# Two no-op instructions in GpSimd's program, behind the identity

## The chip, the cores and the metric

One core of one Trainium2 chip. The metric is the device time of one execution in microseconds (us). Beside it, each run lists the span, from the first to the last recorded instruction.

## The reference

A rotary embedding on a tensor of 16 x 512 x 1024, split into 16 heads of 64. The tables cos and sin are 512 x 32.

```python
def reference(x, cos, sin, num_heads):
    batch, seq, dim = x.shape
    x = x.reshape(batch, seq, num_heads, dim // num_heads)
    x1, x2 = x[..., :half], x[..., half:]            # half = 32
    # ... cos and sin get axes for batch and head
    return np.concatenate([x1 * cos - x2 * sin, x1 * sin + x2 * cos], axis=-1)
```

## The kernel before

The batch is cut into 8 tiles of 4 MiB (128 partitions, 8 rows of 1024 each). SyncE issues all transfers. For seven rows of eight, the product with cos is made by VectorE and the one with sin by GpSimd; for the eighth row VectorE makes both. The sum is made by VectorE for three pairs of rows, and by TensorE and ScalarE for the other two rows. The order on each engine is fixed by hand. What the change and the argument touch:

```python
    load(0, 0, FIRST[0])                              # rows 0 to 2 of the first tile
    # ... tabs is a buffer of the pool "b"
    nc.sync.dma_start(out=sin_sb, in_=sin_v)
    nc.sync.dma_start(out=cos_sb, in_=cos_v)
    # ... the rest of tile 0, tiles 1 to 4
    ident = fixed.tile([P, P], FP32)
    make_identity(nc, ident)                          # GpSimd; the change comes behind this
    zero = fixed.tile([P, BANK], BF16)
    # ... spread is made of ident, TensorE spreads the tables over the partitions
    nc.tensor.matmul(out=sin_t, lhsT=spread, rhs=sin_sb, start=True, stop=True)
    nc.tensor.matmul(out=cos_t, lhsT=spread, rhs=cos_sb, start=True, stop=True)
    # ...
    nc.vector.tensor_scalar_mul(out=sns[:, :, 0, :], in0=sin_k, scalar1=-1.0)
    nc.vector.tensor_copy(out=sns[:, :, 1, :], in_=sin_k)
    # ... in sin_product, GpSimd's only work from here on:
        nc.gpsimd.tensor_tensor(out=o, in0=i, in1=sb, op=ALU.mult)
    # ...
    def stores(t):
        if t == 4:
            store_two(3)
        elif t != 3:
            store(t)
        if t == 2:
            load(5)
            load_two(6)                               # tiles 6 and 7
```

## Time and profile before

| | before |
|---|---|
| time, median of 3 runs | 162.64 us (162.54 to 163.0) |
| time and span of the profiled run | 162.73 and 160.5 us |
| transfers | 67.24 MB, 98.0% of 16 engines' span |
| VectorE, GpSimd busy | 85%, 79% |
| GpSimd idle before its first product | 8.40 us |

The first lines to read are shown in the prediction. One more view, two lines of VectorE's part of the list of waits (who waited for whom: us in total, times, longest):

```profile
DVE x L195 <- POOL b L171: 1.5, 1, 1.5
DVE own_ps L147 <- DMA x<-in_x_dram: 0.4, 1, 0.4
```

Once its first products run, VectorE waits twice: once for a product of GpSimd at 21 us, and once, for 0.4 us, for the last load (tiles 6 and 7). The timeline puts that second one at 111 us:

```profile
111.43 1.23 DVE L147 TENSOR_TENSOR own_ps<-x,tab 128x1024 f32<-128x1024 f32 x1 [0.43 <-DMA x<-in_x_dram]
```

From there to its end at 147.87 VectorE has no wait at all.

### The profile page before, as it was taken

The numbers are of one execution on the slowest core, as the hardware profiler recorded it, in microseconds if no ns is written. First come the engines' busy times: TensorE is split into PE (matmuls) and PEld (weight loads), VectorE is DVE, ScalarE is ACT, GpSimd is POOL, SyncE is SP. The second block draws the span as 40 slices with busy tenths as digits, with TensorE's granted clock in tenths as the row PEclk, the third lists the DMA queues.
The fourth block names the chain that finished last, engine by engine and source line by source line (L and its number), as shares of the span: only waits on it lengthen the run. The fifth ranks groups of instructions, "written<-read, shape, count | busy, mean of one in ns | idle before, by whom it ended". The sixth has DMA issues, their size and how long they took to land.

```text
span 160.5 us, 429 instructions
## 1 busy us (share of the span) xinstructions
PE 60.8 (38%) x71; PEld 18.9 (12%) x71; DVE 136.3 (85%) x85; ACT 18.8 (12%) x25; POOL 126.9 (79%) x38
## 2 busy tenths in 40 slices
PE   3043904074505740393109330844057502922000
PEld 0112201030102100120003000300021101210000
DVE  1079879999999999999999999998999999998000
ACT  0003211003100300021101210031003010211000
POOL 1059999999999999988998699982999999960000
PEclk9999995558655675558555955586556755585555
DMA  5999999999999999999999999999999999999993
GB/s 178 410 413 469 392 490 425 392 465 449 392 433 465 408 392 506 408 392 484 425 400 441 465 400 425 474 400 408 490 408 400 474 433 400 465 433 408 433 465 147
DMA packets 2561, 67.25 MB, mean 419 GB/s; under 512 B 256, under 2 KB 384, under 8 KB 384
## 3 DMA queue, kind: packets, MB, share of 16 engines
q1 hardware_dynamic: 2560, 67.24, 98.0%
q14 instruction: 1, 0.01, 0.0%
HBM read 33.69 MB, written 33.55 MB: 419 GB/s over the span
## 4 chain that ended last, share of the span: by engine, by line
DVE 43%; DMA 34%; issue 7%; POOL 7%; PE 1%; SPq 0%; DVEq 0%
DVE x L195 21%; DVE pd L147 18%; DMA x<-in_x_dram 18%; DMA out_dram<-x 12%; POOL b L171 7%; DMA b<-in_sin_dram 4%; DVE pe_ps L147 2%; PE pd L119 1%; DVE sns L122 0%; SPq L77 0%; DVE sns L123 0%; DVE own_ps L147 0%; DVE x L156 0%; DVEq L195 0%; SPq L80 0%
## 5 line engine op out<-in xcount | busy, mean ns | idle before, releaser
L171 POOL TENSOR_TENSOR b<-x,sns 128x2048 f32<-128x2048 f32 (+1 forms) x32 | 126.2, 3980 | 15.5 <-DVE sns L123 8.4
L195 DVE TENSOR_TENSOR x<-pd,b 128x2048 f32<-128x2048 f32 x24 | 54.9, 2286 | 2.3 <-POOL b L171 1.5
L147 DVE TENSOR_TENSOR pd<-x,tab 128x2048 f32<-128x2048 f32 x24 | 55.0, 2291 | 0.2
L182 PE MATMUL own_ps<-x,ident 128*128 128x512 f32 x32 | 30.2, 1099 | 54.9 <-DVE x L156 50.0
L182 PE MATMUL pe_ps<-b,ident 128*128 128x512 f32 x32 | 28.7, 1001 | 23.4 <-DVE pe_ps L147 23.4
L182 PEld LDWEIGHTS own_ps<-x,ident 128*128 128x128 f32 x32 | 9.4, 324 | 74.5 <-DVE x L156 60.6
L215 ACT COPY x<-own_ps 128x1024 f32<-128x1024 f32 x8 | 8.1, 1012 | 75.0 <-PE own_ps L182 75.0
L187 ACT COPY x<-pe_ps 128x512 f32<-128x512 f32 x16 | 9.4, 586 | 37.6 <-PE pe_ps L182 37.6
L182 PEld LDWEIGHTS pe_ps<-b,ident 128*128 128x128 f32 x32 | 8.1, 278 | 42.7 <-DVE pe_ps L147 34.1
L147 DVE TENSOR_TENSOR pe_ps<-x,tab 128x512 f32<-128x512 f32 x16 | 11.0, 686 | 0.0
L147 DVE TENSOR_TENSOR own_ps<-x,tab 128x1024 f32<-128x1024 f32 x8 | 9.8, 1224 | 0.5 <-DMA x<-in_x_dram 0.4
L156 DVE TENSOR_TENSOR x<-x,tab 128x1024 f32<-128x1024 f32 x8 | 9.7, 1213 | 0.0
L122 DVE TENSOR_SCALAR sns<-pd 128x256 f32<-128x256 f32 x1 | 0.4, 425 | 7.3 <-PE pd L119 7.3
L119 PE MATMUL pd<-b,spread 64*128 64x256 f32 x2 | 1.2, 696 | 5.0 <-DMA b<-in_sin_dram 5.0
L215 ACT ACT_TABLE_LOAD x1 | 1.3, 1283 | 14.6 <-DVE x L156 14.6
L107 PE MATMUL own_ps<-zero 128*128 128x512 bf16 x2 | 1.0, 618 | 1.2 <-DVE zero L103 1.2
L119 PEld LDWEIGHTS pd<-b,spread 64*128 64x128 f32 x2 | 0.5, 307 | 5.9 <-issue 5.9
L120 PE MATMUL tab<-b,spread 64*128 64x256 f32 x2 | 1.1, 631 | 0.0
L103 DVE MEMSET zero<- 128x256 uint32 x1 | 0.3, 272 | 0.9 <-PEq L246 0.9
L120 PEld LDWEIGHTS tab<-b,spread 64*128 64x128 f32 x2 | 0.7, 333 | 0.2
L107 PE MATMUL pe_ps<-zero 128*128 128x512 bf16 x1 | 0.6, 631 | 0.0
L107 PEld LDWEIGHTS <-zero 128*128 128x128 bf16 x3 | 0.3, 123 | 1.5 <-DVE zero L103 1.2
(9 smaller groups left out, 1.8 us busy)
## 6 DMA issues: line engine op xcount, KB each, us to landing
out_dram<-x SPq DMA_DIRECT2D x6, 4096.0 KB, 22.1
x<-in_x_dram SPq DMA_DIRECT2D x2, 8192.0 KB, 38.8
x<-in_x_dram SPq DMA_DIRECT2D x3, 4096.0 KB, 27.9
out_dram<-x SPq DMA_DIRECT2D x1, 8192.0 KB, 33.2
x<-in_x_dram SPq DMA_DIRECT2D x1, 2560.0 KB, 11.4
x<-in_x_dram SPq DMA_DIRECT2D x1, 1536.0 KB, 6.4
b<-in_sin_dram SPq DMA_DIRECT2D x1, 64.0 KB, 6.3
b<-in_cos_dram SPq DMA_DIRECT2D x1, 64.0 KB, 6.1
```

Source lines behind the costliest of these rows:

```text
L103: nc.vector.memset(zero, 0.0)
L107: nc.tensor.matmul(out=ps, lhsT=zero[:, :P], rhs=zero, start=True, stop=True)
L119: nc.tensor.matmul(out=sin_t, lhsT=spread, rhs=sin_sb, start=True, stop=True)
L120: nc.tensor.matmul(out=cos_t, lhsT=spread, rhs=cos_sb, start=True, stop=True)
L122: nc.vector.tensor_scalar_mul(out=sns[:, :, 0, :], in0=sin_k, scalar1=-1.0)
L147: nc.vector.tensor_tensor(out=o, in0=i, in1=cb, op=ALU.mult)
L156: nc.vector.tensor_tensor(out=heads(r), in0=heads(r), in1=s, op=ALU.mult)
L171: nc.gpsimd.tensor_tensor(out=o, in0=i, in1=sb, op=ALU.mult)
L182: nc.tensor.matmul(out=ps, lhsT=ident, rhs=other, start=False, stop=True, skip_group_check=True)
L187: nc.scalar.copy(out=r, in_=pe_ps)
L195: nc.vector.tensor_tensor(out=r, in0=ps, in1=b, op=ALU.add)
L215: nc.scalar.copy(out=r0, in_=own_ps)
```

## The change

It adds two instructions that compute nothing. As its intent one can read: a small pause of GpSimd, to see whether its place in time matters.

```diff
     ident = fixed.tile([P, P], FP32)
     make_identity(nc, ident)
+    for _ in range(2):
+        nc.gpsimd.nop(hint="pause")
     zero = fixed.tile([P, BANK], BF16)
```

## The prediction

> **What bounds the kernel now.** I read the summary first, then the slices of the transfer engines, then the waits of the engine that gets the new instructions, then the chain to the end. The summary and the slices:
>
> ```profile
> span 160.5 us, 429 instructions
> PE 60.8 (38%) x71; PEld 18.9 (12%) x71; DVE 136.3 (85%) x85; ACT 18.8 (12%) x25; POOL 126.9 (79%) x38
> ...
> DMA  5999999999999999999999999999999999999993
> ...
> q1 hardware_dynamic: 2560, 67.24, 98.0%
> ```
>
> What to see: the row "DMA" is in its top tenth in 38 of 40 slices, and the one data queue fills 98.0% of the span of all 16 transfer engines. The kernel reads 32 MiB and writes 32 MiB, plus small tables: 67.24 MB. I cut the span into stretches to get a rate without head and tail: 433 GB/s from 10 to 148 us. 67.24 MB at 433 GB/s is 155.3 us, and the span is 160.5. So about 5 us of the span is head (transfers begin between 1 and 2 us and run at a reduced rate until 3) and tail (nothing moves after 159). The time is the data volume at a flat rate, with one important companion: VectorE, which is busy for 136.3 us and nearly without a gap from 10 us to 147.9. It finishes the last tile at 147.9, the last store of 4 MiB is issued then, and 4.19 MB at 433 GB/s are 9.7 us of the 12.6 that remain. The transfer share in 148 to 157 us is still 0.97. So the two arrive at the end together: the queue has hardly any backlog when VectorE is done, and a real delay of VectorE late in the program would be seen in the time.
>
> Now GpSimd, whose program is the only one changed. Its timeline around the place of the change (start, length, line, operation, and in brackets how long it was idle and for what):
>
> ```profile
> 0.73 0.20 POOL masks.py:197 MEMSET ident<- 128x128 f32 x1 [0.29 <-POOLq L246]
> 1.01 0.29 POOL masks.py:199 TENSOR_SCALAR_AFFINE_SELECT ident<-ident 128x128 f32<-128x128 f32 x1
> 9.71 47.26 POOL L171 TENSOR_TENSOR b<-x,sns 128x2048 f32<-128x2048 f32 x12 [8.40 <-DVE sns L123]
> ```
>
> The identity is done at 1.30 us. The next GpSimd instruction starts at 9.71, and all 8.40 us between are a wait for VectorE's copy of the sine table. Why that comes so late is in the chain:
>
> ```profile
> 1.17 6.34 DMA b<-in_sin_dram
> 7.51 0.14 issue
> 7.64 1.20 PE pd L119 x2
> 8.85 0.02 issue
> 8.87 0.42 DVE sns L122
> 9.30 0.34 DVE sns L123
> 9.64 0.07 issue
> 9.71 4.14 POOL b L171
> ```
>
> The sine table lands 6.34 us after its issue, TensorE spreads it over the partitions, VectorE makes the negated and the plain half, and 0.07 us later GpSimd starts. GpSimd has no part in this chain between 1.30 and 9.64 us. The identity itself is an early input of it (VectorE copies it into the spreading matrix at 1.34 us, for 0.22 us), but that copy is ready at 1.56 and TensorE needs it only at 7.6.
>
> [...] The trace of the kernel before has no such instruction[...]. [...] The nearest thing in the trace is SyncE's semaphore instructions that did not have to wait: 17 to 28 ns. [...]
>
> **The change part by part.** It removes nothing and moves nothing. I compared the two programs as built, on every engine: TensorE, VectorE, ScalarE and SyncE have the same instructions in the same order with the same waits, but for the line numbers, which rise by two. GpSimd's listing gains one row, two no-ops between the identity's select and the first sine product. The waits of every later product are those of before; the no-ops wait for nothing and nothing waits for them.
> - Cost on GpSimd's sequencer: 2 times 17 to 28 ns from the row above, so 34 to 56 ns. If a no-op cost ten times that[...] it would be 0.6 us.
> - What lies in the way: they run after 1.30 us, or even earlier, as the sequencer may be ahead of the engine, and are over by 1.4 us (1.9 in the tenfold case). GpSimd has nothing to do before 9.64 us. Spare time: 8.40 us against 0.06. It would take about 8.40 / 0.028 = 300 such no-ops to fill the gap.
> - What comes out on the path: 0.00 us. The sum is the time of before, 162.64 us.
>
> **The rivals.**
> First: the no-ops delay the first sine product, because they hold the sequencer until the engine is empty or the sequencer reaches the wait late. For it: VectorE does depend on these products (it waited 1.5 us for one at 21 us). Against it: the gap is 150 times the cost. Should it go so, and the whole tenfold cost of 0.6 us came after 9.64, VectorE would be 0.6 us later from 21 us on. 0.43 us of that would go into its own wait for a load at 111 us, if the loads stayed in place, and up to 0.2 us would reach the end, 162.8; if the loads moved along, 163.2.
>
> Second: two more instructions move the rest of GpSimd's program in instruction memory[...]. Against it: GpSimd has 38 counted instructions[...], no jump back, and the profile shows one single packet on the instruction queue in the whole span (0.01 MB). If there were one more fetch in the busy stretch, I would give it 1 to 2 us by the time scale of the small table transfers (6 us, most of it behind other data) with most of it hidden: 163 to 164.
>
> Third: a shift of the phase between GpSimd and the other engines, or of the order in which loads and stores mix. It could go either way. For it: the kernel is tightly tied, with loads that wait for stores (17.4 us of waits on SyncE's side) and VectorE without slack. Against it: all start moments after 9.7 us derive from the sine table's transfer, which SyncE issues at 1.17 us, and no instruction of SyncE is changed. I put it at no more than 0.3 us in either direction, the same as the spread of the three runs of before.
>
> Fourth: faster. Nothing is removed, and with transfers at 98% of the span there is no room for 2% (3.3 us) but in head and tail, which no-ops don't shorten.
>
> **How the range and the chances follow.** The centre is the time of before, set a little up, 162.7, as its three runs (162.54, 162.64, 163.0) lean upwards. The range has to hold only the spread of runs and of a different chip or day: the three runs span 0.46 us, and I give that amount below and a bit more above, because every rival but the fourth adds time: 162.2 to 163.4. A change of over 2% needs 3.25 us either way, over five times the largest size in the first rival; I leave 1% for faster and 1.5% for slower, for a mechanism that I have not thought of.
>
> **What would show it right or wrong.** Right: in the profile of the changed kernel GpSimd's first sine product still starts at about 9.7 us, its idle time before is still put to VectorE's copy of the sine table at about 8.4 us (less the no-ops, if they are counted as busy), and the transfers fill about 98% of a span of 160 to 161 us. Wrong by the first rival: the wait before the first product is put to GpSimd's own queue or "issue", or the product starts over 0.2 us after VectorE's copy ends. Wrong by the second: a second packet on the instruction queue, or a gap in GpSimd's products that no semaphore explains. Wrong by the third: the first product at 9.7 us as before, but VectorE's waits or the stores' moments later in the program differ by more than half a microsecond. If the time differs by over 1% while all of these views are unchanged, the cause lies outside the program as I read it.

No term of its sum went with them: it came to 162.64 us of before plus 0.00 us, with the centre set at 162.7 and the range at 162.2 to 163.4. The 34 to 56 ns for the pair are an estimate from SyncE's semaphore instructions in the trace of before (17 to 28 ns), which are another instruction on another engine; the tenfold case is an assumption. That the two cost sequencer time only was not shown by then; the profile after shows it. Of the argument against an additional fetch, the single packet on the instruction queue is what the trace shows.

## The result, and the profile after

| | before | changed |
|---|---|---|
| time, median of 6 runs | 162.66 us (162.54 to 163.0) | 162.54 us (162.15 to 162.79) |
| ratio, 95% interval | | 0.9987 (0.9969 to 1.0005) |
| time and span of the profiled run | 162.73 and 160.5 us | 162.79 and 161.0 us |

A ratio is the mean time of one kernel's fast runs over that of the other's of the same rounds, so not quite the ratio of the medians. The record marks a run as slow when it is over 1.5% above the fastest of the same kernel; no run is, so every comparison is of fast runs. The page of the changed kernel has these lines in the place of those shown in the prediction:

```profile
span 161.0 us, 431 instructions
PE 56.8 (35%) x71; PEld 18.2 (11%) x71; DVE 136.4 (85%) x85; ACT 18.7 (12%) x25; POOL 126.9 (79%) x38
...
DMA  5999999999999999999999999999999999999993
...
q1 hardware_dynamic: 2560, 67.24, 97.7%
q14 instruction: 1, 0.01, 0.0%
```

Two instructions more, everything else as before; still one packet on the instruction queue. (TensorE's busy time is 4 us lower; its ends are modelled, its count is the same, and it has 1% of the chain that ended last.) The view by source line shows the new instructions (count, then shortest, median and longest in ns, then first and last start in us):

```profile
L103 POOLq NOP  x2: 13/13/13, 1.0 to 1.0; - x2
```

They are booked on GpSimd's sequencer (POOLq), 13 ns each, at 1.0 us, and the view lists nobody who waited for them. GpSimd's timeline:

```profile
1.01 0.29 POOL masks.py:199 TENSOR_SCALAR_AFFINE_SELECT ident<-ident 128x128 f32<-128x128 f32 x1
9.93 47.26 POOL L173 TENSOR_TENSOR b<-x,sns 128x2048 f32<-128x2048 f32 x12 [8.62 <-DVE sns L125]
```

The select starts at 1.01 and lasts 0.29 us, so the no-ops (at 0.98 and 1.03 us) ran beside it. The first product waits for VectorE's copy as before. It is 0.22 us later, and the chain tells why:

```profile
1.17 6.56 DMA b<-in_sin_dram
7.73 0.14 issue
7.86 1.20 PE pd L121 x2
```

The sine table took 6.56 us instead of 6.34 to land. That is a difference of the two executions: every step behind it has the length of before. At the other end, VectorE resumes at

```profile
111.86 1.23 DVE L149 TENSOR_TENSOR own_ps<-x,tab 128x1024 f32<-128x1024 f32 x1 [0.63 <-DMA x<-in_x_dram]
```

0.43 us later than before, and the span is longer by about that much. The profiled run of the changed kernel was its slowest of six, though; its median is lower than that of before. A longer span in the profile and a shorter time in the runs is the first hint that span and time do not go together here.

### The profile page after: what moved, and what is told of

It is laid out like the page before. It is cut to its first block, busy times and chain, and to the rows that moved or that the text cites. A ratio compares the mean times of both kernels' runs of the same rounds, so it can differ in the third digit from the quotient of the medians.

```text
span 161.0 us, 431 instructions
## 1 busy us (share of the span) xinstructions
PE 56.8 (35%) x71; PEld 18.2 (11%) x71; DVE 136.4 (85%) x85; ACT 18.7 (12%) x25; POOL 126.9 (79%) x38
## 4 chain that ended last, share of the span: by engine, by line
DVE 43%; DMA 34%; issue 7%; POOL 7%; PE 1%; SPq 0%; DVEq 0%
DVE x L197 21%; DVE pd L149 18%; DMA x<-in_x_dram 18%; DMA out_dram<-x 12%; POOL b L173 7%; DMA b<-in_sin_dram 4%; DVE pe_ps L149 2%; PE pd L121 1%; DVE sns L124 0%; SPq L77 0%; DVE sns L125 0%; DVE own_ps L149 0%; DVE x L158 0%; DVEq L197 0%; SPq L80 0%
## 5 line engine op out<-in xcount | busy, mean ns | idle before, releaser
L184 PE MATMUL pe_ps<-b,ident 128*128 128x512 f32 x32 | 24.8, 866 | 22.4 <-DVE pe_ps L149 22.4
L184 PEld LDWEIGHTS pe_ps<-b,ident 128*128 128x128 f32 x32 | 7.4, 253 | 42.9 <-DVE pe_ps L149 34.3
L217 ACT ACT_TABLE_LOAD x1 | 1.3, 1283 | 14.8 <-DVE x L158 14.8
```

Of the source, the lines that this page charges most:

```text
L184: nc.tensor.matmul(out=ps, lhsT=ident, rhs=other, start=False, stop=True, skip_group_check=True)
L217: nc.scalar.copy(out=r0, in_=own_ps)
```

## The experiments

My theory: the no-ops vanish in the 8.4 us for which GpSimd waits anyway. Rivals: they cost a fetch of instructions; they shift something else; there is a small real gain or loss. Twelve kernels were run. All gave correct results. The dial for a longer delay is the number of plain no-ops.

### The same kernel twice

No edit: the kernel before against itself.

> The kernel before, unchanged, against itself. Both theories: ratio 1.000 with an interval that holds 1, within 0.3% either way. It measures what this comparison calls a difference when there is none. If the ratio is off by 0.15% or more, the 0.13% by which the changed kernel came out faster is shown to be of the size of noise.

Measured: 162.97 us against 162.79, ratio 1.0009 (0.9996 to 1.0022). So 0.1% is nothing. In its profile the sine table came early and the first product started at 9.52 us, but VectorE resumed at 111.91 and the span was 161.0: an early start alone does not give an early end.

### 600, 800 and 1000 no-ops

```diff
-    for _ in range(2):
+    for _ in range(600):        # 800, 1000
```

> 600 no-ops in the place of the two. One of the two took 13 ns in the trace of the changed kernel, so 600 take 7.8 us and end at about 8.8 us, still before the 9.64 us at which the sine table is ready. Theory (hidden in the wait): first sine product still at 9.7 to 10.0 us, idle before it still put to VectorE's copy, time 162.2 to 163.2, ratio within 0.3% of 1. Rival (instruction fetch[...]): more than one packet on the instruction queue, and the product late by 1 us or more, or a gap between no-ops; time 163.5 or more.

> 800 no-ops: 10.4 us at 13 ns, end at 11.4 us, 1.7 us after the sine table is ready. Theory A (GpSimd's start is on a chain of work that VectorE passes to the end): first product at 11.4, VectorE later by 1.7 us from the first sum on, 0.4 to 0.6 us of it taken up by its own wait for a load at 111 us, end later by 1.1 to 1.3: about 163.9, ratio 1.007 to 1.008. Theory B (the transfers are the bound and have a backlog until the last store): time as before, ratio within 0.3%.

> 1000 no-ops: 13.0 us at 13 ns, end at 14.0 us, 4.3 us after the sine table is ready. Theory A: first product at 14.0, end later by 4.3 less 0.4 to 0.6, about 166.4, ratio 1.022 to 1.024. Theory B: the backlog takes up at least half of it, time under 164.8. If both 800 and 1000 cost nothing, the wait at GpSimd's start is not on the path at all.

| no-ops | first product starts | time, median | ratio |
|---|---|---|---|
| 600 | 26.74 us | 178.24 us | 1.0945 (1.0930 to 1.0960) |
| 800 | 35.52 us | 186.65 us | 1.1464 (1.1446 to 1.1482) |
| 1000 | 43.76 us | 195.21 us | 1.1989 (1.1973 to 1.2006) |

My expectations, from 13 ns per no-op, were wrong by 15 us for 600, and under theory A by 23 us for 800 and 29 us for 1000. The timeline of the 600:

```profile
26.74 35.98 POOL L173 TENSOR_TENSOR b<-x,sns 128x2048 f32<-128x2048 f32 x9 [25.43 <-issue]
```

The product is no longer released by VectorE but by "issue": GpSimd's own sequencer had not got there yet. A stretch of the chain tells how the time is spent (start, length, what):

```profile
8.54 0.01 POOLq L103
8.55 0.03 issue
8.59 0.03 issue
8.63 0.40 issue
9.05 0.03 issue
```

A no-op has 0.01 us of recorded duration, but the next one starts 0.04 us after it. The trace's start times give 40 ns from one to the next (median, in all of these runs; 45 ns from the first to the second). The mistake was to multiply the duration; what counts for these no-ops in series is the distance of their starts. On top of it there is a longer gap at every 128th no-op, from the 55th on, here 0.40 us at 8.63. In the starts of the three runs these gaps measure 0.33 to 0.41 us, once 0.57 and once 0.94. The instruction queue of the 600 fetched more, too:

```profile
q14 instruction: 6, 0.05, 0.1%
```

six packets against one; each is 8192 bytes in the trace's records, and in the no-op stretch they come 5.1 to 5.5 us apart, as the gaps do (128 times 42.7 ns are 5.5 us). One gap ties the two together: the one behind the 183rd no-op, at 8.6 us, has four lengths in four runs. Each time it ends 1.62 to 1.64 us after the packet before it started:

| no-ops | packet starts | gap starts | gap | packet's start to the gap's end |
|---|---|---|---|---|
| 600 | 7.42 us | 8.62 us | 0.41 us | 1.62 us |
| 1000 | 7.56 us | 8.61 us | 0.57 us | 1.62 us |
| 220 | 7.69 us | 8.61 us | 0.69 us | 1.62 us |
| 800 | 7.91 us | 8.61 us | 0.94 us | 1.64 us |

(The 220 follow below.) The later the packet, the longer the gap (0.41 us for the one at 7.42, 0.94 for the one at 7.91), with its end 1.62 to 1.64 us behind the packet's start: I read that as a wait for the fetch. At the later gaps of the 600 the packets started 1.5 to 1.8 us before the gap, and about 0.33 us remained; the first gap, at 3.1 us, has no packet before it in the span and 0.37 to 0.40 us. So rival two is real for long series: packets come, and as often as they do a gap of 0.33 to 0.41 us per 128 no-ops, more where the packet is late (up to 0.94). What the 0.3 us that remain even behind an early packet are, the trace does not say. The gaps are the smaller part of 600 no-ops: 599 distances of 42.7 ns (mean, gaps included) are 25.6 us.

Whether a late start passes through was answered too. The product of the 600 starts 17.2 us later than in the kernel before (26.74 against 9.52), and its runs have a mean span of 176.38 us against 160.66, so 15.7 us more. For 1000 it is 34.2 and 32.7. All but 1.5 us arrive, about three times the 0.4 to 0.6 that theory A allowed to be lost, and theory B (a backlog takes up half) falls. In the profiles of the 600 and the 1000 VectorE has no wait for the last load any more; in the profile of the kernel before of the same call that wait was 1.10 us, so it is most of what was lost.

### 150 and 220 no-ops: the edge of the gap

The same edit with 150 and 220.

> 150 no-ops. The long series showed that a no-op of GpSimd takes 40 ns from start to start (13 ns are recorded), plus about 0.3 us at every 128th. From 1.0 us, 150 end at 1.0 + 150 * 0.0427 = 7.4 us, before the sine table is ready (9.4 to 9.85). Pitch theory: first product unmoved (9.5 to 9.95), released by VectorE's copy, ratio within 0.25% of 1. Rival (a no-op costs the end something wherever it stands): 150 * 42.7 ns = 6.4 us, ratio 1.04.

> 220 no-ops end at 1.0 + 220 * 0.0427 = 10.4 us, 0.5 to 0.9 us after the table is ready. Pitch theory: first product at 10.3 to 10.7, released by the sequencer (issue). For the end there are two theories. Reset (VectorE's wait at 111 us for a load of the saturated transfers takes the delay up): that wait, 0.4 to 1.1 us before, shrinks by the delay, and the end moves by no more than 0.3 us, ratio within 0.2% of 1. Pass-on (a late start goes through to the end): +0.5 to +0.9 us, ratio 1.003 to 1.006.

For 150, the last no-op starts at 7.28 us, the first product at 9.63, and VectorE releases it:

```profile
9.63 47.27 POOL L173 TENSOR_TENSOR b<-x,sns 128x2048 f32<-128x2048 f32 x12 [8.33 <-DVE sns L125]
```

162.72 us, ratio 0.9997 (0.9979 to 1.0014): hidden by this ratio, as the theory of the 40 ns says (the spans, below, leave a question). For 220, the last starts at 10.75 (a gap of 0.69 us among them), and

```profile
10.92 47.29 POOL L173 TENSOR_TENSOR b<-x,sns 128x2048 f32<-128x2048 f32 x12 [9.61 <-issue]
```

163.75 us, ratio 1.0055 (1.0041 to 1.0069). The product is 1.2 to 1.5 us later than in the profiles of kernels with few no-ops or none (9.42 to 9.71, that of the changed kernel apart), and the mean span is 161.95 us against 160.65: the whole delay arrives. So the edge lies between 150 and 220, and of the two theories on the end, "reset" falls and "pass-on" holds. How it passes on is seen at the last load:

```profile
113.01 1.23 DVE L149 TENSOR_TENSOR own_ps<-x,tab 128x1024 f32<-128x1024 f32 x1 [0.79 <-DMA x<-in_x_dram]
```

VectorE's wait there did not shrink. The load moved along: it landed 1.1 to 1.7 us later than in the other profiles. It was issued at 83.41 us, where the others have 82.2 to 82.6, because SyncE waits for an earlier store, which waits for VectorE (its list of waits from 60 to 85 us: 17.3 us in two waits of the loads for stores, 16.5 and 14.8 us of the stores for VectorE). In a table by stretches of one us around the last store (columns: stretch, its length, busy time of PE, PEld, DVE, ACT and POOL with counts, clock, transfer share, GB/s), the transfers of the kernel before

```profile
148.00:149.00 1.00, 0.00 (x0) 0.00 (x0) 0.00 (x0) 0.00 (x0) 0.00 (x0) 0.50 0.92 393
149.00:150.00 1.00, 0.00 (x0) 0.00 (x0) 0.00 (x0) 0.00 (x0) 0.00 (x0) 0.50 0.69 295
```

do not run dry (in the second profile of the same kernel, whose load landed 0.5 us later, the two shares are 0.08 and 1.14), while those of the 220

```profile
148.00:149.00 1.00, 0.00 (x0) 0.00 (x0) 1.00 (x1) 0.00 (x0) 0.00 (x0) 0.50 0.16 66
149.00:150.00 1.00, 0.00 (x0) 0.00 (x0) 0.46 (x1) 0.00 (x0) 0.00 (x0) 0.50 0.00 0
```

nearly stop for over a us: no packet is under way and VectorE (DVE, the third busy column) is still at its last sum. That is where the lost time shows. Why the load lands later although the same 47.5 MB have been moved by 112 us after the first transfer in both kernels is only half answered. All that was issued up to and with this load is 46.3 MB. When VectorE resumed, 46.6 to 46.8 MB of packets had ended in the other eight profiles, and 47.2 MB here. So some 0.5 MB more of the store issued behind the load had gone ahead of the load's last part. Why, stays open: the trace does not tell which engine moved which part.

### Two no-ops before each of the 32 products

```diff
+        for _ in range(2):
+            nc.gpsimd.nop(hint="pause")
         nc.gpsimd.tensor_tensor(out=o, in0=i, in1=sb, op=ALU.mult)
```

(against the kernel before)

> Two no-ops before every one of the 32 sine products, 64 in all. Hidden (the sequencer runs them while the product before is still at work): GpSimd's first twelve products last 47.26 us as before (47.2 to 47.4) and the ratio is within 0.25% of 1. Serial (they come between products): 12 * 0.08 = 1.0 us more, 48.2 us; the first sum of the second pair, which waits for GpSimd, comes 0.24 us later, and the time is up to 0.3 us more.

Measured: 162.32 us, ratio 0.9968 (0.9953 to 0.9983).

```profile
9.44 47.28 POOL L173 TENSOR_TENSOR b<-x,sns 128x2048 f32<-128x2048 f32 x12 [8.13 <-DVE sns L123]
```

The twelve products last 47.28 us as before, so the no-ops between them are hidden: the sequencer runs them while a product is at work. In the chain of this run four no-ops start at 13.58 to 13.83 us, between the start of the first product at 9.44 and that of the second at 13.90; from start to start that is 4.46 us, against 4.47 before. This run has two packets on the instruction queue, at 72.7 and 76.4 us, against one before, and the time is not longer for it. It is even 0.3% lower than that of before, outside what was expected, and the interval leaves out 1.

### The changed kernel again, and comment lines only

```diff
     make_identity(nc, ident)
+    # a line
+    # a line
```

> The changed kernel again, two no-ops, on this call's chip. All theories: ratio 0.998 to 1.002. If the first comparison's 0.9987 was noise, this one has no reason to lie below 1 again; if it does so with an interval that leaves out 1, a small real gain has to be explained.

> The kernel before with two comment lines where the no-ops stand: the same instructions, other line numbers. Control. Both theories: ratio 0.998 to 1.002. If it comes out at 0.996 to 0.998, as the changed kernel did the last time, then those 0.3 to 0.4% belong to the comparison of two loaded programs and not to no-ops.

> The changed kernel a third time. Noise theory: a ratio between 0.998 and 1.002 that has no fixed sign over the three calls (0.9987, 0.9964 so far). Gain theory (the two no-ops save something small): 0.996 to 0.998 again, while the control with comment lines stays at 1.000. In the profile, noise theory expects no step between the sine table and the first product that is shorter than before.

| kernel | time, median | ratio |
|---|---|---|
| two no-ops, second time | 162.25 us | 0.9964 (0.9950 to 0.9978) |
| two no-ops, third time | 162.44 us | 0.9978 (0.9961 to 0.9994) |
| comment lines only | 162.78 us | 0.9998 (0.9984 to 1.0012) |

The sign is the same three times and the control stays at 1, so the noise theory falls: there is a small real gain. It is not in the span. I took the span (given to 0.1 us) from the time, run by run:

| kernels | runs | time less span |
|---|---|---|
| before | 31 | 2.13 to 2.27 us |
| no no-ops: same kernel, comment lines, and the two below | 21 | 2.17 to 2.26 us |
| no-ops: 2 (three times), 150, 220, 600, 800, 1000, 2 per product | 48 | 1.76 to 1.86 us |

The two groups do not touch. With no-ops, whatever their number, 0.40 us less lies outside the recorded instructions. The spans themselves agree: with two no-ops they are 160.68, 160.46 and 160.67 us on the mean, before 160.66, 160.65 and 160.61. And 0.40 of 162.8 us is 0.25%, where the three ratios have a mean of 0.9976. So the gain is shown to lie before the first or after the last recorded instruction, and to come with the presence of no-ops and not with line numbers. One more transfer instruction on SyncE, in the last kernel below, does not bring it. What it is there, nothing in the traces tells: first and last recorded instructions are the same, at the same distances. All tried numbers were even, and all no-ops on GpSimd; whether another extra instruction on GpSimd would do the same is open.

This also corrects the reading of 150 and 220. The mean span of 150 is 161.02 against 160.65 us, which the 0.4 us outside hides in the ratio. Its runs spread from 160.7 to 161.5, those of the kernel before and of the pair from 160.3 to 161.1, and in the profile its product is not late, so I leave open whether that is an effect of 150 no-ops. For 220, 1.30 us more span and 0.41 less outside make the 0.9 us between the mean times.

### The tables through another queue, and the last store in two

```diff
-    nc.sync.dma_start(out=sin_sb, in_=sin_v)
-    nc.sync.dma_start(out=cos_sb, in_=cos_v)
+    nc.scalar.dma_start(out=sin_sb, in_=sin_v)
+    nc.scalar.dma_start(out=cos_sb, in_=cos_v)
```

> No no-ops; the two table loads go through ScalarE's queue instead of SyncE's, so they are issued beside the first load and not behind it. The first product should start 1 us or more before 9.5 us. Bound theory (the span is the moment at which VectorE resumes at 111 us, plus 49.1 us, and the stream of transfers fixes that moment unless the start is late): resumption still at 111.3 to 112.0, VectorE's wait there grows by as much as the start was early, ratio 0.997 to 1.002. Chain theory (the start passes through in both directions, as 1.2 us of delay gave 0.9 us): 0.8 us or more gained per us, ratio 0.995 or less.

Measured: 163.80 us, ratio 1.0061 (1.0047 to 1.0075). The premise fell: the tables did not come earlier but later. The table of issues, before and then here (size, us to landing):

```profile
b<-in_sin_dram SPq DMA_DIRECT2D x1, 64.0 KB, 6.3
b<-in_cos_dram SPq DMA_DIRECT2D x1, 64.0 KB, 6.1
```

```profile
b<-in_sin_dram ACTq DMA_DIRECT2D x1, 64.0 KB, 7.3
b<-in_cos_dram ACTq DMA_DIRECT2D x1, 64.0 KB, 11.1
```

Issued through ScalarE, at 0.74 and 1.30 us, they have a queue of their own (q10: 160 packets, 0.13 MB) and run beside the loads of x, issued from 0.74 us on; before, all of those but the first had stood behind them, issued from 2.37 us on. Why the tables land later that way, no run here isolates. VectorE waited 3.4 us for its cos table, the wait for the last load vanished, and the end was VectorE's:

```profile
148.00:149.00 1.00, 0.00 (x0) 0.00 (x0) 1.00 (x1) 0.00 (x0) 0.00 (x0) 0.50 0.16 66
149.00:150.00 1.00, 0.00 (x0) 0.00 (x0) 0.89 (x1) 0.00 (x0) 0.00 (x0) 0.50 0.00 0
```

the same dry stretch as with 220 no-ops. So the run does not test an early start, but it shows again that a late VectorE (its end at 149.89 us against 147.87 before) is paid for at the last store. The last kernel also stores six of the eight rows of the last tile early:

```diff
+        if t == NT - 1:
+            cut = (KK - 2) * dim
+            nc.sync.dma_start(out=out_v[t][:, :cut], in_=tiles[t][:, :cut])
     # ... and in stores(t), for the last tile:
+            nc.sync.dma_start(out=out_v[t][:, cut:], in_=tiles[t][:, cut:])
```

> As the run before it, and the last tile is stored in two parts: six of its eight rows once they are done, two at the end. The transfers ran dry for 0 to 0.4 us before the last store in the profiles so far, and after it, so filling that gap can give 0.0 to 0.4 us, and a smaller last store shortens nothing if the queue is full: ratio against the run before it 0.997 to 1.000. Rival (the last store's 11.7 us from issue to landing are on the path and shrink with its size): a gain of several us, ratio 0.97 to 0.98.

Measured: 162.94 us, ratio 0.9999 to the kernel before (0.9984 to 1.0013); over the run above, mean times of 162.88 and 163.85 us, 0.994. That is more than the 0.0 to 0.4 us expected, because the gap to be filled was larger than in the profiles I had looked at:

```profile
148.00:149.00 1.00, 0.00 (x0) 0.00 (x0) 1.00 (x1) 0.00 (x0) 0.00 (x0) 0.50 0.82 352
149.00:150.00 1.00, 0.00 (x0) 0.00 (x0) 0.65 (x1) 0.00 (x0) 0.00 (x0) 0.50 0.91 393
```

With work in the queue, a VectorE that ends 1.8 us later than in the kernel before (149.65 against 147.87) costs nothing: the mean spans are 160.65 and 160.61 us. The rival (several us) fell: the last store, of 1 MiB, took 10.3 us to land, and the one of 4 MiB had taken 11.7, so most of that time is not its own size.

## Why the prediction was right or wrong

- **The bound.** Right, and sharper now. In nine profiles (before, the changed kernel three times, the same kernel, comment lines, 150, 220 and two per product) the span less the moment at which VectorE resumes for the last load is 49.0 to 49.2 us. From 111 us on the program is rigid; the span varies with that load's landing.
- **The cost of the pair.** The conclusion holds, the size was off. I took 17 to 28 ns per no-op from SyncE's semaphore instructions, 34 to 56 ns for two. Measured: 40 to 45 ns from start to start, so about 0.09 us. "About 300" to fill the gap was too many: 150 fit, 220 were 1.2 us late or more. At 42.7 ns it takes 200 to get from 1.0 to 9.6 us.
- **"What comes out on the path: 0.00 us."** Right for the span: the pair's three mean spans (160.46 to 160.68 us) are those of before (160.61 to 160.66) within 0.2 us. The mechanism, a wait that hides them, is shown by 150 no-ops, which end at 7.3 us with the release still put to VectorE, and by 220, which do not fit and are paid for. That the mean span of 150 is 0.37 us longer is the open point above.
- **First rival, delay of the first product.** Rightly put aside for two; it is what happens from 220 on. Of my two versions (VectorE's wait takes it up, or the loads move along) the second is what the run with 220 shows (VectorE still waits 0.79 us); with 600 to 1000 the wait is used up, and the rest comes out at the end.
- **Second rival, instruction fetch.** Absent for two (one packet in both profiles), there for hundreds: six packets for 600, with a gap of 0.33 to 0.41 us at each 128th no-op, up to 0.94 where the packet came late. The 1 to 2 us that I gave to one more fetch in the busy stretch did not show: two no-ops per product brought a second packet and no delay.
- **Third rival, a shift of phase.** In the profiled run VectorE resumed 0.43 us later and the span was 161.0 us; the unchanged kernel's spans reach from 160.3 to 161.0. No effect of the change is to be seen. (In the range I wrote that "every rival but the fourth adds time"; this one could go either way by its own words.)
- **Fourth rival, faster.** Here a step failed in small: the room for a gain was sought "in head and tail, which no-ops don't shorten", both inside the span. The kernels with no-ops have 0.40 us less outside the span. The median came out at 162.54 and not at the centre of 162.7, and my upward lean had the sign of the only real effect wrong. That the range held the result owes to the 0.46 us given to the spread of runs, not to a foreseen gain; a second comparison of the same kernel came to 162.25 us, near the lower edge. The gain's mechanism stays open.

## What to carry to other kernels

Cost an instruction of a sequencer by the distance of its start to the next start, not by its recorded duration (for the no-ops here 40 ns against 13), and then compare that with the wait it falls into: 0.09 us in a wait of 8.4 us is nothing, but the same instruction 220 times is on the path. A queue of transfers that is busy all along (98.0% here) did not by itself absorb a delay where loads wait for stores and stores for the engine that is late: 220 no-ops made the first product 1.2 to 1.5 us late and the span 1.30 us longer. Look whether the queue runs dry before the last store, as it did there (shares of 0.16 and 0.00). Where a ratio of a few parts in a thousand comes again with the same sign, split the time into span and rest before looking for a cause inside the span.
